# Fourier tables fetched during the fold, padded tails, softmax scaling on GpSimd, merge weights a tile ahead

## The chip, the cores and the metric

The kernel runs on one core of one Trainium2 chip. The metric is the device time of one execution in microseconds (us). A core has TensorE (PE, matrix products), VectorE (DVE), ScalarE (ACT), GpSimd (POOL) and SyncE (SP), which work side by side and wait for each other by semaphores. DMA transfers are issued from the queues of SP, ACT and POOL. Matrix products land in PSUM banks; GpSimd can't read these.

## What is computed

One layer of a transformer-like encoder over two sequences with shared weights: 1024 sample tokens and 256 prompt tokens, each with 16 learned meta tokens in front, width 1024.

```python
h = rms_norm(x, norm_mix_g)
q, k, v, f, g_attn, g_four = split(h @ w_in)       # 512, 128, 128, 512, 1024, 1024
q, k = axial_rope(head_rms_norm(q)), axial_rope(head_rms_norm(k))
a = softmax(q @ k.T * HEAD_DIM ** -0.5) @ v @ w_attn_o   # 8 query heads share 2 key heads
fo = real(fftn(f, axes=(positions, group channels), norm='ortho')) @ w_four_o
x = x + (sigmoid(g_attn) * a + sigmoid(g_four) * fo) @ w_out
x = x + (silu(gate) * up) @ w_ffn_out              # gate, up = rms_norm(x) @ w_ffn_in
return rms_norm(x, final_norm_g)                   # without the meta tokens
```

## The kernel before

Nearly every product of two matrices is done as three products of rounded parts: each operand is split into a high part (ScalarE copies it into a rounded format) and a low part (the difference, made by VectorE or GpSimd), and `three` (L224 to L231) adds high x high, high x low and low x high. So every fresh operand costs one copy and one subtraction before TensorE can use it, and these splits must stay ahead of TensorE.

On-chip memory is handed out by `Slots`: 27 single slots and 7 triples. A freed slot goes to the back of a line and the one freed longest ago is handed out first. A new holder's first writer waits for the old holder's last reader.

The order of the work. Up to the attention's start the framework orders the instructions of each engine itself, by the order in the program and its own estimate of the times. In attention, merge and the projection's start the order of TensorE, ScalarE and VectorE is the program's (`manual_schedule`), while that of GpSimd is still the framework's. Each engine runs its list strictly in order.

The stages that the change touches:

- **Fold.** The real Fourier transform uses the symmetry of cosine and sine: `folds` (L461) adds and subtracts mirrored positions of the normed input, for eight blocks k of 128 channels. GpSimd rebuilds the input from its parts (L488), VectorE makes sums and differences (L491, L492), and both are split (L494, L495) into the slots called eo.
- **Fourier input.** `fourier_in` (L500) multiplies the eight folded blocks with channel weights into six PSUM banks (L515 to L519): four banks of 128 positions, one of 41 and one of 128, the last and 9 rows of the fifth belonging to the prompt. Then ScalarE and VectorE split the banks into ue and uo (L539 to L545), bank after bank.
- **Position tables.** `fourier` (L611) multiplies ue and uo with tables of cosines and sines over positions: tabp for the prompt (fp, two tables of 128 and 41 rows, L649), then tabc and tabs for the sample (fs, five tables each, of 128, 128, 128, 128 and 9 rows, L666). There are five kinds of output (two blocks of cosines, a narrow one of four columns, two blocks of sines), with one half for fp and two halves for fs. The tables are fetched by DMAs on GpSimd's queue (L615, L672).
- **Gates as filler.** `gate_gen` (L553) computes the gate logits in groups: 12 weight units, and for each eight steps of three matmuls of 512 columns. `weave` (L146) mixes it with the main work: each `yield` of the main work names a cost in nominal ns, a share of it is added to a debt, and gate groups (a nominal 640 each for the first 512 positions) are emitted until it is paid. In `build` the shares are 0.6 in the Fourier stage, 0.35 in `q_pass` (queries) and 0.7 in `kv_pass` (keys and values). The gates of the other positions fill attention, with a cost per step in the table `FILL` (L551): "p" for the prompt's tiles, "s" for the sample's, "end" and "drain" for the last.
- **Attention.** Ten tiles of 128 queries in two groups of four heads; the two prompt tiles come first. For each head: scores into PSUM (L949), maximum on VectorE (L954), exponential on ScalarE with the row's sum (L961). One head later VectorE makes the reciprocal of the sum (L965) and scales the row (L966). From one head after the end of a group the rows are transposed on TensorE (L883), split (L885, L886) and multiplied with V (L903, L904).
- **Merge.** For each of eight tiles of 128 output channels: `need` (L1085) combines and splits the tile's weights, `fourier(i)` (L1106) makes the Fourier product one tile ahead of the attention product (loop from L1166), and both are joined with the sigmoid of the gates. The weights' DMAs are issued by `load` on SP.
- **Output projection.** `w_out` (L1218) is started by `next(then)` from inside the merge; its first weight unit is split at L1253, the low part by GpSimd.

After these come the second norm and the feed-forward network, which the change leaves as they are.

Of the kernel before, what the change touches and what calls it, by code (L numbers as in the profile page):

```python
# [10 lines left out]
F32R = mybir.dt.float32r  # L11
AF = mybir.ActivationFunctionType
ALU = mybir.AluOpType
# [4 lines left out]
P = 128  # L18
# [118 lines left out]
def f32(ap):  # L137
    return ap.bitcast(F32)
# [44 lines left out]
class Kernel:  # L183
# [313 lines left out]
            yield  # L497
        sl.put(*hs, ep, od)

    def fourier_in(self, ps):  # L500

        nc, sl = self.nc, self.sl
        cols = [(j * P, P) for j in range(4)] + [(512, 41), (553, P)]
        banks = [ps.tile([P, 512], F32, tag="mm" if j < 4 else "tr", name=f"u{j}") for j in range(6)]
        for k in range(KD):
            while k not in self.eo:
                next(self.fold)
            parts = self.eo.pop(k)
            w = [x[:, k % 2 * 512 : k % 2 * 512 + 512] for x in self.wc[k // 2]]
            for j, (b, m) in enumerate(cols):  # L510
                for odd, (h, l) in enumerate(parts):
                    s = slice(260, 512) if odd else slice(260)
                    out, hm, lm = banks[j][:m, s], h[:, b : b + m], l[:, b : b + m]
                    if k or odd:
                        nc.tensor.matmul(out, hm, w[0][:, s], start=False, stop=False)  # L515
                    else:
                        nc.tensor.matmul(banks[j][:m, :], hm, self.wz[:], start=True, stop=False)
                    nc.tensor.matmul(out, hm, w[1][:, s], start=False, stop=False)
                    nc.tensor.matmul(out, lm, w[0][:, s], start=False, stop=odd == 1 and k == KD - 1)  # L519
                yield 0  # L520
            for x in parts:
                sl.put(*x)
            if k + 2 < KD:
                next(self.fold)
            if k % 2:
                sl.put(*self.wc[k // 2])
        next(self.fold, None)
        ue = [sl.get("ue", F32R) for _ in range(3)]
        uo = [sl.get("uo", F32R) for _ in range(3)]
        for x in uo:  # L530
            nc.gpsimd.memset(f32(x.v(4, 256))[:, :, 252:256], 0.0)
        for j, (_, m) in enumerate(cols):
            ev = banks[j][:m, :260].rearrange("p (g c) -> p g c", g=4)
            b = j % 2 * 520
            u = ue[j // 2]
            for base, w, src in ((0, 64, ev[:, :, :64]), (256, 1, ev[:, :, 64:65])):
                hv = u.v(4, w, b + base)[:m]
                lv = u.v(4, w, b + 260 + base)[:m]
                nc.scalar.copy(hv, src)  # L539
                nc.vector.tensor_tensor(lv, src, f32(hv), op=ALU.subtract)  # L540
            b = j % 2 * 512
            u = uo[j // 2]
            src = banks[j][:m, 260:512]
            nc.scalar.copy(u[:m, b : b + 252], src)
            nc.vector.tensor_tensor(u[:m, b + 256 : b + 508], src, f32(u[:m, b : b + 252]), op=ALU.subtract)  # L545
        self.U = ue, uo
        yield 6000

    FILL = {"s": 455, "p": 350, "end": 480, "drain": 900}  # L551

    def gate_gen(self, chunks, lo_engine):  # L553

# [56 lines left out]
    def fourier(self, ps):  # L611
        nc, a, sl = self.nc, self.a, self.sl
        tp = [sl.get(f"tabp{j}", F32R) for j in range(2)]
        for j, m in enumerate((P, 41)):
            nc.gpsimd.dma_start(tp[j][:m, : 4 * NLP], a["pos_p"][j, :m])  # L615
        yield from self.fourier_in(ps)
        us = self.U

        def u_e(uu, j, m, p, part):
# [24 lines left out]
            nc.sync.dma_start(self.f_d[row : row + m, lo : lo + n], st[:m, :n])  # L644


        ms = [P, 41]
        for kind, p in kinds:
            rows = 4 if kind == "4" else P  # L649
            pf = ps.tile([P, 512], F32, tag="mm", name=f"fp{kind}{p}")  # L650
# [12 lines left out]
        sl.put(*tp)  # L663


        ms = [P, P, P, P, 9]  # L666
        tabs = {}

        def tab(name):
            tabs[name] = [sl.get("tab" + name, F32R) for _ in range(5)]  # L670
            for j, m in enumerate(ms):
                nc.gpsimd.dma_start(tabs[name][j][:m, :1040], a["pos_" + name][j, :m])  # L672

        tab("c")
        for i, (kind, p) in enumerate(kinds):
            if i == 1:
                tab("s")
            rows = 4 if kind == "4" else P
            tt = tabs["s" if kind == "o" else "c"]
            st = sl.get("fst")  # L680
# [170 lines left out]
    def attention(self, ps, tiles, tag_s, tag_v):  # L851
# [80 lines left out]
        for i, (t, g) in enumerate(units):  # L932
# [8 lines left out]
            for h in range(4):  # L941
# [21 lines left out]

                def scale(p=p, rc=rc, total=total):
                    nc.vector.reciprocal(rc, total)  # L965
                    nc.vector.tensor_scalar(p, p, rc, None, op0=ALU.mult)  # L966

                ps4.append(p)
                turns(1)
# [88 lines left out]
    def merge(self, then):  # L1058
# [105 lines left out]
        load(2)  # L1164
        load_gates(2)
        for i in range(8):  # L1166
            yield from fourier(i + 1)
            if i == 0:
                run_all(self.last_af)
# [7 lines left out]
            for c in (0, 2, 1):  # L1177
# [11 lines left out]
                    self.three(pm[:, :n], [(wk, mv)], k == 0, k == 3)  # L1189
                    yield 3 * n / 2.4  # L1190
                if c == 0:
                    need(i + 2)
                    load(i + 3)
                v = gt[:, n : 2 * n]
                nc.vector.tensor_tensor(v, pm[:, :n], v, op=ALU.mult)
# [8 lines left out]
                    sl.put(gt)  # L1204

                late.append(rows)
                if c == 2 and i == 7:
                    next(then)
            sl.put(w)
            if i < 4:  # L1210
# [7 lines left out]
    def w_out(self, tiles, ps, then=None, apart=False):  # L1218
# [31 lines left out]
        raw = sl.get("wo", F32, "s")  # L1250
        nc.sync.dma_start(raw[:, :1024], a["w_out"][0])
        yield 0
        units[0] = self.split(raw, 1024, "wo", nc.gpsimd, "s")  # L1253
        sl.put(raw)
        yield 0
        for half in range(2):
# [438 lines left out]
    def build(self):  # L1695
# [3 lines left out]
        with self.psum("pb", {"mm": 4, "tr": 2, "g": 2}) as ps:  # L1699
# [4 lines left out]
            def ahead(main, start, then):  # L1704
                for i, cost in enumerate(main):
                    if i == start:
                        next(then)
                    yield cost

            weave(ahead(self.fourier(ps), QSTART, q_pass), gates, 0.6)  # L1710
            weave(ahead(q_pass, KVSTART, kv_pass), gates, 0.35)
            weave(kv_pass, gates, 0.7)
            run_all(gates)
            self.free_hT(self.hT[0])
            gates = Filler(self.gate_gen([1, 2], self.nc.gpsimd))
# [193 lines left out]
```

## Time and profile before

| | |
|---|---|
| runs | 1735.22, 1735.85, 1737.88 us (median 1735.85) |
| the profiled execution | 1737.35 us, of which the span from first to last instruction is 1735.6 |
| mean granted TensorE clock | 0.988 of full speed |
| bytes moved | 195.77 MB, mean 113 GB/s |

How to read it: times count from the span's start. PE is TensorE's matmuls, PEld its weight loads, which overlap them; matmuls are pipelined, so starts, not lengths, tell the pace. A line's shape such as `9*128 9x260` is the stationary operand (9 rows, 128 columns) and the moving one (9 rows, 260 columns). A bracket in the order of time holds how long the engine stood before the instruction, and what ended that. In a row of waits stand the engine and line that waited, for whom, the us in total, the times and the longest. Tile names are those that the memory had first, so a table may be shown under the name of an earlier tile in the same triple. L numbers are lines of the kernel.

### The profile page before, as it was taken

The numbers are of one execution on the slowest core, as the hardware profiler recorded it, in microseconds if no ns is written. First come the engines' busy times: TensorE is split into PE (matmuls) and PEld (weight loads), VectorE is DVE, ScalarE is ACT, GpSimd is POOL, SyncE is SP. The second block draws the span as 40 slices with busy tenths as digits, with TensorE's granted clock in tenths as the row PEclk, the third lists the DMA queues.
The fourth block names the chain that finished last, engine by engine and source line by source line (L and its number), as shares of the span: only waits on it lengthen the run. The fifth ranks groups of instructions, "written<-read, shape, count | busy, mean of one in ns | idle before, by whom it ended". The sixth has DMA issues, their size and how long they took to land.

```text
span 1735.6 us, 25870 instructions
## 1 busy us (share of the span) xinstructions
PE 1672.8 (96%) x9789; PEld 1489.0 (86%) x9789; DVE 1137.2 (66%) x2086; ACT 723.0 (42%) x1462; POOL 299.7 (17%) x347
## 2 busy tenths in 40 slices
PE   7998999999999999989989999999999999999998
PEld 7897888877787878878879999999999998888886
DVE  5562454357888886652379766667666768665685
ACT  6432333355666666451355222222232224444444
POOL 3440233311002111663353000000000000000002
PEclk9997999999999999999999999999999999999999
DMA  6124232221111217534442222322232237553534
GB/s 245 39 106 134 100 122 91 80 79 57 44 59 45 67 56 231 169 108 143 150 166 77 86 69 95 102 90 83 94 102 90 70 119 256 196 182 101 159 98 152
DMA packets 90541, 195.77 MB, mean 113 GB/s; under 512 B 9773, under 2 KB 41161, under 8 KB 90416
## 3 DMA queue, kind: packets, MB, share of 16 engines
q1 hardware_dynamic: 80592, 176.88, 31.0%
q10 hardware_dynamic: 8400, 12.53, 2.0%
q0 software_dynamic: 1424, 4.70, 0.8%
q8 instruction: 77, 1.26, 0.3%
q14 instruction: 48, 0.39, 0.1%
HBM read 138.65 MB, written 55.42 MB: 112 GB/s over the span
## 4 chain that ended last, share of the span: by engine, by line
PE 60%; DVE 6%; issue 3%; ACT 3%; POOL 2%; DMA 1%; POOLq 0%; ACTq 0%; SPq 0%; DVEq 0%
PE i L231 10%; PE i L229 10%; PE i L230 10%; PE o L231 5%; PE o L230 5%; PE o L229 4%; PE S L949 3%; PE pt L883 2%; PE wo L230 1%; PE pv L903 1%; PE wo L231 1%; PE wo L229 1%; PE pv L904 1%; PE g L229 1%; POOL gt L1196 1%
## 5 line engine op out<-in xcount | busy, mean ns | idle before, releaser
L1402 ACT CAST w<-wi 128x512 fp32r<-128x512 f32 x168 | 104.0, 621 | 270.5 <-PE i L231 216.5
L229 PE MATMUL i<-A,w 128*128 128x384 f32 x616 | 208.6, 339 | 3.0 <-ACT w L1402 2.7
L231 PE MATMUL i<-A,w 128*128 128x384 f32 x616 | 208.4, 339 | 2.4 <-POOL w L1404 2.3
L230 PE MATMUL i<-A,w 128*128 128x384 f32 x616 | 208.2, 338 | 0.0
L229 PE MATMUL i<-Ah,w 128*128 128x256 f32 x616 | 173.6, 282 | 0.9 <-DVE sc L1458 0.7
L231 PE MATMUL i<-Ah,w 128*128 128x256 f32 x616 | 173.7, 282 | 0.0
L230 PE MATMUL i<-Al,w 128*128 128x256 f32 x616 | 173.3, 281 | 0.0
L238 POOL TENSOR_SCALAR fin0r<-fin0ss 128x1 f32<-128x1 f32 x1 | 0.8, 785 | 757.5 <-ACT X L246 757.5
L885 ACT CAST pT<-pt 128x512 fp32r<-128x512 f32 x156 | 90.5, 580 | 89.6 <-PE pt L883 87.6
L886 DVE TENSOR_TENSOR pT<-pt,pT 128x512 fp32r<-128x512 f32 x156 | 106.9, 686 | 26.9 <-ACT pT L885 25.1
L1404 DVE TENSOR_TENSOR w<-wi,w 128x512 fp32r<-128x512 f32 x154 | 105.3, 685 | 29.0 <-ACT w L1402 28.6
L229 PEld LDWEIGHTS i<-A,w 128*128 128x128 f32 x616 | 116.7, 190 | 3.6 <-ACT w L1402 2.9
L231 PEld LDWEIGHTS i<-A,w 128*128 128x128 f32 x616 | 116.5, 189 | 3.1 <-POOL w L1404 3.1
L229 PEld LDWEIGHTS i<-Ah,w 128*128 128x128 f32 x616 | 116.3, 189 | 1.6 <-DVE sc L1458 0.9
L230 PEld LDWEIGHTS i<-Al,w 128*128 128x128 f32 x616 | 116.5, 189 | 0.0
L230 PEld LDWEIGHTS i<-A,w 128*128 128x128 f32 x616 | 116.5, 189 | 0.0
L231 PEld LDWEIGHTS i<-Ah,w 128*128 128x128 f32 x616 | 116.4, 189 | 0.0
L954 DVE TENSOR_REDUCE sm<-S 128x1 f32<-128x1040 f32 (+1 forms) x80 | 86.4, 1080 | 41.0 <-PE S L949 35.1
L961 ACT ACTIVATE p<-S,sm 128x1040 f32<-128x1040 f32 (+1 forms) x80 | 80.1, 1001 | 35.3 <-DVE sm L954 30.9
L883 PE MATMUL pt<-ident,p 128*128 128x128 f32 (+1 forms) x624 | 93.7, 273 | 0.0
L231 PE MATMUL o<-wfo,act 128*128 128x512 f32 (+1 forms) x212 | 82.2, 388 | 1.6 <-DVE act L1536 1.6
L230 PE MATMUL o<-wfo,act 128*128 128x512 f32 (+1 forms) x212 | 82.1, 387 | 0.2 <-DVE wfo L1540 0.2
(734 smaller groups left out, 4470.5 us busy)
## 6 DMA issues: line engine op xcount, KB each, us to landing
wi<-w_fi SPq DMA_DIRECT2D x48, 512.0 KB
act_d<-sc SPq DMA_DIRECT2D x77, 192.0 KB
wg<-w_g SPq DMA_DIRECT2D x24, 512.0 KB
act<-act_d SPq DMA_DIRECT2D x37, 320.0 KB
wfo<-w_fo SPq DMA_DIRECT2D x21, 512.0 KB
X<-act_d SPq DMA_DIRECT2D x31, 320.0 KB
act_d<-sc SPq DMA_DIRECT2D x77, 128.0 KB
gt<-gate SPq DMA_DIRECT2D x32, 256.0 KB
```

Of the source, the lines that this page charges most:

```text
L229: mm(out, sh, mh, start=first and i == 0, stop=False)
L230: mm(out, sh, ml, start=False, stop=False)
L231: mm(out, slo, mh, start=False, stop=last and i == n - 1)
L883: nc.tensor.transpose(pt[:rows, h * P : (h + 1) * P], me.ps4[h][:, col : col + rows], self.ident[:])
L885: nc.scalar.copy(pT[:rows, :512], pt[:rows, :])
L886: nc.vector.tensor_tensor(pT[:rows, 512:1024], pt[:rows, :], f32(pT[:rows, :512]), op=ALU.subtract)
L903: nc.tensor.matmul(me.pv[:], vst, pT[:rows, :512], start=j == 0, stop=False)
L949: nc.tensor.matmul(S[:, base + lo : base + hi], hq, self.kT[seq][g][v][:, lo:hi], start=v == 0, stop=v == 1)
L954: nc.vector.tensor_reduce(nb, S[:, base : base + L], axis=AX.X, op=ALU.max, negate=True)
L961: self.last_exp = nc.scalar.activation(p, S[:, base : base + L], AF.Exp, bias=nb, accum_out=total)
L1402: nc.scalar.copy(w[:, :512], src)
L1404: eng.tensor_tensor(w[:, 512:1024], src, f32(w[:, :512]), op=ALU.subtract)
```

## The change

- The gates' first unit is loaded and split before the fold begins (`next(gates)`); the shares become 0.6, 0.28 and 0.62, and the last yield of `fourier_in` grows from 6000 to 8000.
- The ten sample tables are fetched from within the fold loop, as slots come free, instead of after `fourier_in`.
- The two short tables and the short bank are filled with zeros up to 128 rows, and their matmuls use all 128.
- `FILL`: "s" from 455 to 420, "p" from 350 to 500.
- The scaling of the exponentials moves from VectorE to GpSimd; the reciprocal stays.
- In the merge `need(i + 2)` is called before `fourier(i + 1)` instead of after the first product of tile i; in the last tile the first projection unit is split after the first product instead of the second, with its low part on VectorE.

```diff
@@ fourier_in
-    def fourier_in(self, ps):
+    def fourier_in(self, ps, tab):
...
             if k + 2 < KD:
                 next(self.fold)
+            elif k + 2 == KD:
+                next(self.fold, None)
+            for _ in range((0, 0, 2, 0, 2, 0, 4, 2)[k]):
+                tab()
             if k % 2:
                 sl.put(*self.wc[k // 2])
-        next(self.fold, None)
         ue = [sl.get("ue", F32R) for _ in range(3)]
         uo = [sl.get("uo", F32R) for _ in range(3)]
-        for x in uo:
+        for x in uo[:2]:
             nc.gpsimd.memset(f32(x.v(4, 256))[:, :, 252:256], 0.0)
+        nc.gpsimd.memset(f32(ue[2][:, :520]), 0.0)
+        nc.gpsimd.memset(f32(uo[2][:, :1024]), 0.0)
...
-        yield 6000
+        yield 8000
-    FILL = {"s": 455, "p": 350, "end": 480, "drain": 900}
+    FILL = {"s": 420, "p": 500, "end": 480, "drain": 900}
@@ fourier
-        for j, m in enumerate((P, 41)):
-            nc.gpsimd.dma_start(tp[j][:m, : 4 * NLP], a["pos_p"][j, :m])
-        yield from self.fourier_in(ps)
+        for j in range(2):
+            nc.gpsimd.dma_start(tp[j][:, : 4 * NLP], a["pos_p"][j])
+        tabs = {"c": [], "s": []}
+        def tab():
+            name = "c" if len(tabs["c"]) < 5 else "s"
+            j = len(tabs[name])
+            t = sl.get("tab" + name, F32R, "s")
+            tabs[name].append(t)
+            if j == 4:
+                nc.gpsimd.memset(f32(t[:, :1040]), 0.0)
+            m = P if j < 4 else 9
+            nc.gpsimd.dma_start(t[:m, :1040], a["pos_" + name][j, :m])
+        yield from self.fourier_in(ps, tab)
...
-        ms = [P, 41]
+        ms = [P, P]
...
-        ms = [P, P, P, P, 9]
-        tabs = {}
-        def tab(name):
-            tabs[name] = [sl.get("tab" + name, F32R) for _ in range(5)]
-            for j, m in enumerate(ms):
-                nc.gpsimd.dma_start(tabs[name][j][:m, :1040], a["pos_" + name][j, :m])
-        tab("c")
+        ms = [P] * 5
         for i, (kind, p) in enumerate(kinds):
-            if i == 1:
-                tab("s")
@@ attention
-                    nc.vector.tensor_scalar(p, p, rc, None, op0=ALU.mult)
+                    nc.gpsimd.tensor_scalar(p, p, rc, None, op0=ALU.mult)
@@ merge
         for i in range(8):
+            if i:
+                need(i + 2)
             yield from fourier(i + 1)
...
                 if c == 0:
-                    need(i + 2)
+                    if i == 0:
+                        need(2)
                     load(i + 3)
...
-                if c == 2 and i == 7:
+                if c == 0 and i == 7:
                     next(then)
@@ w_out
-        units[0] = self.split(raw, 1024, "wo", nc.gpsimd, "s")
+        units[0] = self.split(raw, 1024, "wo", nc.vector, "s")
@@ build
+            next(gates)
             weave(ahead(self.fourier(ps), QSTART, q_pass), gates, 0.6)
-            weave(ahead(q_pass, KVSTART, kv_pass), gates, 0.35)
-            weave(kv_pass, gates, 0.7)
+            weave(ahead(q_pass, KVSTART, kv_pass), gates, 0.28)
+            weave(kv_pass, gates, 0.62)
```

## The prediction

> **What bounds the kernel now.** I read the page first, then a table of stages, then TensorE's own waits, then the order of time around each hole.
>
> ```profile
> span 1735.6 us, 25870 instructions
> PE 1672.8 (96%) x9789; PEld 1489.0 (86%) x9789; DVE 1137.2 (66%) x2086; ACT 723.0 (42%) x1462; POOL 299.7 (17%) x347
> PEclk9997999999999999999999999999999999999999
> ```
>
> TensorE is busy 96% of the span, and the clock row dips in one slice. An edit can only fill TensorE's idle 63 us, win back halved clock, or shorten TensorE's own work. The table of stages (columns: length, then busy time of PE, PEld, DVE, ACT, POOL, then clock, DMA share, GB/s) shows where these lie.
>
> ```profile
> 127.50:136.30 8.80, 4.34 (x21) 3.24 (x19) 5.55 (x17) 4.80 (x19) 2.64 (x5) 0.95 0.98 336
> 136.30:155.66 19.36, 19.21 (x65) 15.67 (x66) 3.70 (x12) 2.71 (x6) 0.00 (x0) 0.50 0.19 56
> 155.66:336.00 180.34, 178.16 (x1008) 150.63 (x1007) 81.00 (x198) 55.00 (x130) 57.12 (x83) 1.00 0.29 100
> 336.00:343.55 7.55, 4.85 (x18) 3.69 (x19) 3.09 (x14) 2.82 (x11) 1.33 (x3) 0.77 0.68 244
> 400.00:680.00 280.00, 271.64 (x1624) 224.17 (x1625) 231.05 (x345) 180.85 (x327) 37.85 (x33) 1.00 0.23 71
> 777.00:787.30 10.30, 6.34 (x16) 4.75 (x16) 5.50 (x6) 5.11 (x6) 6.79 (x5) 0.67 0.75 257
> 787.30:1735.60 948.30, 931.86 (x5431) 859.23 (x5429) 638.04 (x1167) 331.48 (x640) 75.72 (x67) 0.99 0.37 121
> ```
>
> The diff touches nothing that runs after 787, so the last row stays and every microsecond won earlier arrives at the end. The holes are: before the table matmuls, with 19.36 us at half clock behind it; at the end of the K/V pass (336 to 343.55); thin ones in attention; and the start of the output projection (777 to 787.3). Between 155.66 and 336 TensorE waits for almost nothing, so what is won before it is carried through.
>
> **The hole before the table matmuls.** In order of time (start, length, engine, line, operation, in brackets the wait before it and what ended it):
>
> ```profile
> 126.41 1.14 ACT L571 CAST wgh<-wg 128x512 fp32r<-128x512 f32 x2 [1.65 <-DMA wg<-w_g]
> 126.81 0.29 PE L515 MATMUL u<-wch,eo 128*128 128x260 f32 x1
> 127.46 0.36 ACT L539 CAST ue<-u 128x256 fp32r<-128x256 f32 x1
> 131.44 0.40 PE L231 MATMUL g<-hT0h,wgl 128*128 128x512 f32 x1
> 135.88 0.36 ACT L539 CAST ue<-u 128x256 fp32r<-128x256 f32 x1
> 136.29 0.48 PE L229 MATMUL fpe<-hT0l,ue 128*128 128x136 f32 x1 [4.46 <-ACT ue L539]
> ```
>
> ScalarE copies six banks out from 127.46; the sixth, which the first table matmul needs, starts at 135.88: 8.4 us for five banks, 1.7 each. It starts late because ScalarE stood behind the gate weights' DMA (126.41). The sixth bank's own matmuls begin at 126.81 and end just before 127.7, so a bank takes about 0.7 us on TensorE and the first was complete near 126.81 - 4 x 0.7 = 124.0. With next(gates) the first gate unit is loaded and split before the folds; ScalarE can start near 124.1 and reach the sixth bank near 132.5. TensorE covers the time with gate groups: six ran in about 4.3 us (the busy 4.34 of the first row), 0.7 each. The yield of 8000 x 0.6 = 4800 buys eight of nominal 640, so cover lasts to 127.5 + 5.6 = 133.1. The idle 4.46 us falls to about 0.3: gain 4.2. So short a pause should not halve the clock (400 to 680 has 8.4 us of idle in pieces at clock 1.00), and the 19.36 us at 0.50 shrink by half less what was waiting in them: 9.5.
>
> The price is in the folds: the gates now hold three slots during them, and ten tables take slots as they come free, with their DMA issues and one or two memsets on POOL between its fold additions. More fold splits must then wait for TensorE to release the fold before last. It happens already:
>
> ```profile
> 97.43 0.77 ACT L494 CAST eo<-ep 128x681 fp32r<-128x681 f32 x1 [3.19 <-PE u L518]
> ```
>
> ScalarE waited 3.19 us there and TensorE did not, for it had a whole fold (six banks of 0.7, 4.2 us) in hand. For six folds I bound the cost by 0 and 0.7 each, 0 to 4, and take 0.5. The memsets of the padded ue and uo precede banks five and six only and have over 4 us: nothing. The tables already arrived before they were needed (the 136.29 row waits for ScalarE, not a DMA), so fetching them early gains nothing itself.
>
> **The tails.** The padded operand replaces a 9-row (or 41-row) matmul with one of 128 rows:
>
> ```profile
> 156.16 0.28 PE L231 MATMUL fse<-tabc,ue 128*128 128x260 f32 x1
> 156.28 0.28 PE L229 MATMUL fse<-tabc,ue 128*128 128x260 f32 x1
> ...
> 156.52 0.28 PE L231 MATMUL fse<-tabc,ue 128*128 128x260 f32 x1
> 156.73 0.38 PE L229 MATMUL fse<-tabc,ue 9*128 9x260 f32 x1
> 156.95 0.28 PE L230 MATMUL fse<-tabc,ue 9*128 9x260 f32 x1
> 157.07 0.28 PE L231 MATMUL fse<-tabc,ue 9*128 9x260 f32 x1
> 157.28 0.50 PE L229 MATMUL g<-hT0h,wgh 128*128 128x512 f32 x1
> 157.61 0.40 PE L230 MATMUL g<-hT0h,wgh 128*128 128x512 f32 x1
> ```
>
> Inside the tail the starts are 0.12 apart (156.95 to 157.07), as in full-height runs, so the rows cost nothing; but the step into it is 0.21 and the next 0.22, out of it 0.21 and 0.33 where a 512-column matmul takes 0.23 (0.69 for three). That is 0.09 + 0.10 + 0.09 + 0.10 = 0.38 us per tail. Twelve of the fifteen tails have 128 output columns: 12 x 0.38 = 4.6; I leave the three narrow ones out.
>
> **The end of the K/V pass.**
>
> ```profile
> 339.43 0.33 PE L790 MATMUL ktr<-ident,ks 128*128 128x128 f32 x1 [2.70 <-DVE ks L779]
> ```
>
> Gate work runs out here. There are 96 groups of 640, or 61440. Before, the three shares spend 26000 x 0.6 + 61000 x 0.35 + 34040 x 0.7 = 60778 ahead of the last yield, one group left. After: 28000 x 0.6 + 61000 x 0.28 + 34040 x 0.62 = 54985, ten left, and the last yield of 8000 x 0.62 places seven or eight, 5 us, over the 2.70 us wait. With it goes the half clock (0.77 over 7.55 us is 1.7 us lost). Gain 4.4. In the Q pass each tile gets one fifth less gate work, with no wait next in line.
>
> **Attention.** Four edits meet: scaling moves from VectorE to GpSimd, the filler rate for the short tiles rises 350 to 500, and for the long ones falls 455 to 420 (about 32 x 150 = 4800 against 120 x 35 = 4200 nominal, so the same work earlier).
>
> ```profile
> PE S L949 <- ACT p L961: 6.2, 10, 1.5
> PE pv L903 <- DVE ao L911: 5.2, 9, 0.9
> 482.48 0.15 DVE L965 RECIPROCAL sm<-sm 128x1 f32<-128x1 f32 x1
> 482.73 0.77 DVE L966 TENSOR_SCALAR p<-p,sm 128x1040 f32<-128x1040 f32 x1
> 484.36 0.60 PE L883 MATMUL pt<-ident,p 128*128 128x128 f32 x4
> L1016 POOL CAST pT<-x64r 4x1024 fp32r<-4x1024 f32 x3 | 3.1, 1034 | 15.2 <-DMA x64r<-w 15.1
> L214 POOL TENSOR_TENSOR wol<-wo,woh 128x1024 fp32r<-128x1024 f32 x14 | 34.5, 2472 | 47.0 <-ACT woh L213 46.3 <-issue 0.7
> ```
>
> TensorE is busy 271.64 of 280 us there, so VectorE's 0.77 us less per head can return at most a part of the waits of 6.2 and 5.2 us; both also hang on ScalarE. I take 1 us for these and 0.5 for the fill. The new cost is delay: the reciprocal ends at 482.63, and at a change of unit TensorE wants the scaled row at the transposes of the next head, 484.36: 1.73 us. GpSimd's price for the multiply isn't in the trace; the nearest rows are its one-input cast over 1024 columns, 1.03 us, and its two-input subtraction over 1024, 2.47 us. The multiply has one tensor input, so I take 1.1 to 1.3, inside the 1.73. Behind it on POOL stand the gate weights' low halves, wanted a unit later. Sum for attention 1.5, from +6 down to -12 (next part).
>
> **Merge and output projection.**
>
> ```profile
> PE fo L229 <- ACT wm L1095: 2.5, 4, 0.8
> PE fo L229 <- ACT pT L1095: 0.7, 1, 0.7
> PE fo L231 <- DVE wm L1096: 0.6, 4, 0.2
> PE wo L230 <- POOL wol L214: 2.3, 1, 2.3
> PE wo L229 <- ACT woh L213: 1.7, 1, 1.7
> ```
>
> Between 690 and 777 TensorE waits 3.8 us for split merge weights that are made in the tile before their use. A tile earlier they have a tile's length more (eight tiles in about 90 us): gain 3.5. VectorE and ScalarE may then stand at need() for the weights' DMA, with the sums of the first Fourier half queued behind; four PSUM banks cover that. The first projection unit, split after the first of tile 7's three products and on VectorE, is ready before TensorE ends the merge: 2.3 + 1.7 = 4.0 us go, and the half clock behind: (1 - 0.67) / 0.5 x 10.3 = 6.8 us at half speed, of which TensorE worked about 5.8, 2.9 lost. I keep 6.4 of the 6.9.
>
> **Sum.** 4.2 + 9.5 - 0.5 + 4.6 + 4.4 + 1.5 + 3.5 + 6.4 = 33.6 us. The profiled execution took 1737.35 for a span of 1735.6; the sum gives 1703.8 there. It stands 1.5 above the median of the runs, 1735.85, so the forecast is 1702.
>
> **Rivals.**
> *The first hole only narrows.* If the copies still start near 127.5 (a split of the second gate unit in front, or late slots), cover to 133.1 leaves 3.1 us idle before 136.29, and the clock falls again: 2.8 + up to 9.5 come back, 1712 to 1714. For it: ScalarE did take the second unit's split at 126.41. Against: that load is also issued earlier now. The clock in these rows fell after an idle 2.70 us too. The Trainium skill (TensorE: Matmul & The Clock Gate, Why this matters for your kernels) says that one idle window, gaps over about 3 us, halves the clock; by it 3.1 us would be on the edge and 2.70 safe, and the trace has 0.77 around the 2.70.
> *Scaling is late.* At the two-input 2.47 us it misses the 1.73 by 0.74 in each of 16 long units, 12 us: 1714. The Trainium skill (GPSIMD Engine Reference, Engine selection) says not to do elementwise work there, two-input operations being about half as fast as on VectorE but one-input ones near line rate; by it the multiply would be near the cast's price and the sum would stand, though no row here shows a one-input operation on all 128 rows.
> *The tails gain nothing* if the steps belong to the change of table rather than of height: 1707. Against: the table changes between 156.16 and 156.28 too, at 0.12.
> *POOL's queue turns against it, slower than before.*
>
> ```profile
> POOL wgl L572 <- ACT wgh L571: 207.0, 21, 29.4
> ```
>
> GpSimd stands 207.0 us, 10 at a time, at ScalarE's gate copies. It does so with nothing else to do; but if its fixed order puts such a wait ahead of a unit's last scaling, TensorE stands for most of it. It outweighs the 33.6 from four such waits in twenty units: 1742 with four, 10 us each. Against: the copy is issued within a step of its subtraction.
>
> **Numbers.** Forecast 0.62, narrowed hole 0.15, late scaling 0.11, tails 0.06, queue 0.04, the rest small gains lost together 0.02. Predicted 1702; low end 1692 (waits of attention recovered whole, no cost in the folds, more filler effect), high end 1716 (either of the two large rivals with its price). Faster by over 0.2%, about what measurement can tell: 0.94; slower 0.04; within 0.02.
>
> **What would show it.** Right: no idle over 1 us before the first table matmul and clock 1.00 from 127 to 345; 0.12 steps through the fifth table; no wait at the last K transposes; no wait of fo for wm; the projection's first matmul straight behind the merge. Wrong: a half-clock stretch near 140; transposes waiting for POOL; holes between 100 and 127 in the folds; a GpSimd multiply of 2 us or more.

## The result and the profile after

The changed kernel takes 1760.88 us (median of four runs, 1759.32 to 1762.57), the kernel before 1735.53 beside it: ratio 1.0144, 95% interval 1.0127 to 1.0162. It is 25 us slower; 34 us faster were forecast.

The page of the changed kernel, its span, its busy times and its clock row:

```profile
span 1760.8 us, 26129 instructions
PE 1673.6 (95%) x9789; PEld 1488.5 (85%) x9789; DVE 1090.9 (62%) x2008; ACT 722.3 (41%) x1462; POOL 498.2 (28%) x428
PEclk9999999999999899999999999999999999999999
```

TensorE is busy as long as before (1672.8), so nearly all of the loss is idle time. POOL has gone from 299.7 to 498.2 us, more than four times what VectorE gave up (1137.2 to 1090.9). The table of stages (columns as before):

```profile
130.00:137.00 7.00, 7.00 (x37) 5.85 (x36) 4.92 (x15) 4.39 (x15) 0.52 (x1) 1.00 0.74 217
137.00:157.00 20.00, 19.31 (x137) 16.86 (x137) 4.98 (x12) 3.48 (x7) 0.00 (x0) 1.00 0.43 143
157.00:322.00 165.00, 162.53 (x927) 139.02 (x924) 82.76 (x206) 55.45 (x135) 59.97 (x86) 1.00 0.30 102
323.80:704.30 380.50, 341.32 (x1928) 275.73 (x1929) 209.67 (x340) 210.02 (x395) 247.55 (x120) 0.97 0.21 65
704.30:805.70 101.40, 90.56 (x499) 79.76 (x498) 66.89 (x125) 50.95 (x104) 55.91 (x78) 0.98 0.48 152
805.70:1760.70 955.00, 938.24 (x5444) 864.03 (x5444) 644.86 (x1175) 335.35 (x645) 78.03 (x68) 0.99 0.37 122
```

The front went as forecast: no hole near 130, clock 1.00. The fourth row, attention, has 39.2 us in which TensorE does nothing, and a clock of 0.97. Cut at the first scores, the first Fourier product of the merge and the first projection product, the two spans compare like this:

| stage | before | after | difference | forecast |
|---|---|---|---|---|
| up to the first scores | 340.0 | 323.8 | -16.2 | -22.2 |
| attention | 340.8 | 380.5 | +39.7 | -1.5 |
| merge | 97.9 | 101.4 | +3.5 | -9.9 |
| projection to end | 956.9 | 955.1 | -1.8 | 0 |

What attention waits for (us in total, times, longest), and the price of the multiplication in the groups of lines:

```profile
POOL p L974 <- DVE sm L973: 99.7, 44, 12.0
PE S L957 <- ACT p L969: 16.6, 21, 7.3
PE pt L891 <- POOL p L974: 14.1, 15, 1.2
ACT pT L893 <- POOL wgl L577: 11.1, 2, 8.3
```

```profile
L974 POOL TENSOR_SCALAR p<-p,sm 128x1040 f32<-128x1040 f32 x64 | 187.1, 2925 | 87.5 <-DVE sm L973 74.0 <-PE pt L891 8.4 <-issue 2.9
```

GpSimd takes 2.925 us for what VectorE did in 0.77. One change of unit in order of time:

```profile
483.63 0.15 DVE L973 RECIPROCAL sm<-sm 128x1 f32<-128x1 f32 x1
483.97 2.92 POOL L974 TENSOR_SCALAR p<-p,sm 128x1040 f32<-128x1040 f32 x1 [0.92 <-DVE sm L973]
486.95 0.33 PE L891 MATMUL pt<-ident,p 128*128 128x128 f32 x1 [0.92 <-POOL p L974]
```

The reciprocal ends at 483.78, the multiplication starts 0.19 later, and the transposes start the moment it ends, 0.92 us after they could have.

### The profile page after: what moved, and what is told of

It is laid out like the page before. It is cut to its first block, busy times and chain, and to the rows that moved or that the text cites. A ratio compares the mean times of both kernels' runs of the same rounds, so it can differ in the third digit from the quotient of the medians.

```text
span 1760.8 us, 26129 instructions
## 1 busy us (share of the span) xinstructions
PE 1673.6 (95%) x9789; PEld 1488.5 (85%) x9789; DVE 1090.9 (62%) x2008; ACT 722.3 (41%) x1462; POOL 498.2 (28%) x428
## 4 chain that ended last, share of the span: by engine, by line
PE 59%; DVE 7%; POOL 7%; ACT 4%; issue 4%; DMA 2%; POOLq 0%; DVEq 0%; ACTq 0%; SPq 0%
PE i L231 10%; PE i L229 10%; PE i L230 10%; PE o L231 4%; PE o L230 4%; PE o L229 4%; POOL p L974 4%; PE S L957 3%; PE pt L891 2%; PE wo L230 1%; PE wo L229 1%; PE wo L231 1%; PE pv L911 1%; DVE sm L962 1%; PE g L229 1%
## 5 line engine op out<-in xcount | busy, mean ns | idle before, releaser
L974 POOL TENSOR_SCALAR p<-p,sm 128x1040 f32<-128x1040 f32 (+1 forms) x80 | 202.5, 2532 | 116.5 <-DVE sm L973 99.7
L894 DVE TENSOR_TENSOR pT<-pt,pT 128x512 fp32r<-128x512 f32 (+1 forms) x138 | 94.7, 687 | 90.0 <-ACT pT L893 89.7
L893 ACT CAST pT<-pt 128x512 fp32r<-128x512 f32 (+1 forms) x138 | 80.1, 581 | 109.5 <-PE pt L891 96.0
L891 PE MATMUL pt<-ident,p 128*128 128x128 f32 (+1 forms) x624 | 99.2, 278 | 14.4 <-POOL p L974 14.1
L891 PEld LDWEIGHTS pt<-ident,p 128*128 128x128 f32 (+1 forms) x624 | 74.1, 136 | 29.9 <-POOL p L974 18.0
```

Of the source, the lines that this page charges most:

```text
L891: nc.tensor.transpose(pt[:rows, h * P : (h + 1) * P], me.ps4[h][:, col : col + rows], self.ident[:])
L893: nc.scalar.copy(pT[:rows, :512], pt[:rows, :])
L894: nc.vector.tensor_tensor(pT[:rows, 512:1024], pt[:rows, :], f32(pT[:rows, :512]), op=ALU.subtract)
L974: nc.gpsimd.tensor_scalar(p, p, rc, None, op0=ALU.mult)
```

## The experiments

Differences below are between medians; the median of before moved by 1.2 us from one set of runs to another. The theory was that the price of the multiplication on GpSimd makes the loss in attention; its rivals were the filler rates, and a loss only through lateness at the changes of unit.

**One part back, one part alone.** In the changed kernel the multiplication goes back to VectorE:

```diff
-                    nc.gpsimd.tensor_scalar(p, p, rc, None, op0=ALU.mult)
+                    nc.vector.tensor_scalar(p, p, rc, None, op0=ALU.mult)
```

> The changed kernel with one word put back: the multiplication runs on VectorE again. Theory (the price of the multiplication on GpSimd is what attention lost: 2.92 us against VectorE's 0.77): attention falls from 380.5 us back to the 341 it had before, and the time to 1721 (1760.9 - 39.7). Rival (the new filler rates 420 and 500 starve the long tiles, the multiplication only shifts where it waits): 1750 to 1760, and TensorE goes on waiting in attention. Rival (the multiplication costs only its lateness at the sixteen unit changes, 14 us of waits of the transposes): 1745, and the waits of the scores for the exponentials stay.

Measured: 1726.51 us, 34.4 less than the changed kernel, attention 344.9. The reverse line in the kernel before:

> The kernel before with this one word changed: the multiplication on GpSimd. Theory (price): 1775 (1735.5 + 39.7), attention about 380 us. Rival (filler rates): 1736 to 1745, since the rates are the old ones. Rival (lateness at unit changes only): 1750.

Measured: 1766.04, ratio 1.0177 (1.0162 to 1.0192), attention 371.0. This one line makes the kernel slower by about 30 us by itself, with the old rates; the theory holds, at 30 to 34 us and not 39.7. Two more runs take the rest of the change apart. The merge as before:

```diff
-            if i:
-                need(i + 2)
             yield from fourier(i + 1)
...
-                    if i == 0:
-                        need(2)
+                    need(i + 2)
...
-                if c == 0 and i == 7:
+                if c == 2 and i == 7:
...
-        units[0] = self.split(raw, 1024, "wo", nc.vector, "s")
+        units[0] = self.split(raw, 1024, "wo", nc.gpsimd, "s")
```

> The multiplication on VectorE and the merge as before (weights folded in the tile before, projection unit split on GpSimd after the last product); front stages and filler rates as changed. Theory (the earlier fold of merge weights itself lengthened the merge by the 3.5 us that the trace shows): 3 to 4 us faster than the run with the multiplication on VectorE alone, 1717. Rival (my sum: the fold a tile ahead saves 9.9 us, and only GpSimd's backlog from attention hid it): 10 us slower than that run, 1731.

Measured: 1726.62, the same as with the merge edits (1726.51). Both expectations missed: in the whole the edits neither cost 3.5 nor save 9.9. The stages show why: the merge is longer with them, 102.3 us for 99.1, and what follows it shorter, 954.1 for 956.1. Then the filler rates as before too:

```diff
-    FILL = {"s": 420, "p": 500, "end": 480, "drain": 900}
+    FILL = {"s": 455, "p": 350, "end": 480, "drain": 900}
```

> As the run before it, and the filler rates are the old ones too: what is left of the change is the front (tables during the fold, gates first, shares, padded tails). Theory: the front brings the 16.2 us that the trace shows up to the first scores: 1719. My sum had 22.2 there: 1713. The difference to the run before it is the rates alone: theory nothing (within 2 us); my sum half a microsecond.

Measured: 1720.97 (one of its six runs took 1730.75, the others 1719.28 to 1723.90). The front alone is worth 15.8 us; the rates, which I took for nothing, cost 5.7 (attention 339.8 to 346.5 us). Front -15.8, rates +5.7, merge -0.1, multiplication +34.4 make +24.2, against 25.3 measured. As each part was taken off the run before it, they add up by construction; what is left over is the movement of the median of before. In the kernel before, with nothing else changed, the multiplication cost less, 29.3.

**Late, or too busy?** Only the fourth head of each unit, the last before the transposes, is scaled on VectorE:

```diff
-                def scale(p=p, rc=rc, total=total):
+                def scale(p=p, rc=rc, total=total, e=nc.vector if h == 3 else nc.gpsimd):
                     nc.vector.reciprocal(rc, total)
-                    nc.gpsimd.tensor_scalar(p, p, rc, None, op0=ALU.mult)
+                    e.tensor_scalar(p, p, rc, None, op0=ALU.mult)
```

> The changed kernel with the multiplication of every unit's fourth head on VectorE, the other three heads on GpSimd. Theory (lateness: what costs is that the last row of a unit is scaled too late for the transposes): the waits of the transposes for GpSimd go and nearly all of the 34.4 us between the changed kernel and the one with VectorE come back, 1727 to 1733. Rival (occupancy: GpSimd's queue delays the gate halves and the slots, by as much as it is busy): a quarter of the multiplications goes and so does a quarter of the 34.4, 1752.

Measured: 1737.48. A quarter of the multiplications taken away brought back 23.4 of the 34.4 us, and the transposes no longer wait for GpSimd at all. So two thirds of the loss is lateness of one multiplication in four. Left are 11 us, which neither expectation gave. The stage of attention, with VectorE alone and in this run (columns as before):

```profile
322.90:667.80 344.90, 328.99 (x1928) 268.57 (x1929) 264.67 (x420) 210.55 (x395) 47.03 (x40) 1.00 0.23 72
323.00:676.20 353.20, 330.03 (x1929) 269.42 (x1929) 222.62 (x360) 209.95 (x395) 198.10 (x100) 0.99 0.23 70
```

TensorE is idle for 15.9 us in the first row and 23.2 in the second; in the changed kernel it was 39.2. So the late multiplications made 16.0 us of idle time, 14.1 of them the direct waits, and 11.3 us of busy time (341.3 for 330.0), at a clock of 0.97 for 0.99. The scores wait for the exponentials nearly as long without them, 14.7 us for 16.6 (6.9 with VectorE alone), most of the difference to VectorE in one hole (GpSimd and ScalarE in order of time):

```profile
519.67 2.38 POOL L1027 TENSOR_TENSOR hT0l<-x64r,hT0l 4x1024 fp32r<-4x1024 f32 x1
522.15 2.92 POOL L974 TENSOR_SCALAR p<-p,sm 128x1040 f32<-128x1040 f32 x1
525.04 1.26 POOL L577 TENSOR_TENSOR wgl<-wg,wgh 128x512 fp32r<-128x512 f32 x1
526.33 0.58 ACT L893 CAST pT<-pt 128x512 fp32r<-128x512 f32 x1 [7.21 <-POOL wgl L577]
```

The low half of a gate unit stands behind a multiplication and the Fourier tails (the rows of four that `fourier` leaves over); ScalarE waits 7.21 us for the slot that it frees, and the scores behind it 6.2. The changed kernel has the same hole, 8.3 and 7.3 us. So the tails went to VectorE:

```diff
-                nc.gpsimd.tensor_copy(t[b : b + 4, :], r[b : b + 4, :n])
+                nc.vector.tensor_copy(t[b : b + 4, :], r[b : b + 4, :n])
...
-            nc.gpsimd.tensor_tensor(t[x, :], r[x, :n], f32(t[x, :]), op=ALU.subtract)
+            nc.vector.tensor_tensor(t[x, :], r[x, :n], f32(t[x, :]), op=ALU.subtract)
```

> The kernel with the fourth head's multiplication on VectorE (1737.5), and the eight operations on the 4-row Fourier tails (six casts and two subtractions of 0.75 to 2.4 us, which GpSimd took between 509 and 522 us) on VectorE too. Theory (the 11 us that this kernel still loses to VectorE alone are mostly one hole: the tails push a multiplication and a gate half back, and ScalarE waits 7.2 us for the slot of that half): the hole of 520 to 530 us goes, 6.2 us of wait and about 3 of half clock, 1728. Rival (the loss is spread over all units, with the waits of the scores for the exponentials): 1735 to 1738.

Measured: 1735.12, 2.4 less. The hole at 520 is gone (TensorE busy 17.38 of 520 to 540, where it was 13.41), but attention is 352.6 us long and was 353.2: the time was lost again elsewhere. Of the remaining 8.6 us, 5.3 stand in the trace as waits of the scores for the exponentials, spread out now (12.2 us in 20 waits, none over 2.0; 6.9 in 11 with VectorE alone). Why the exponentials come later stays open.

**What the price is.** The changed kernel with a constant as the factor:

```diff
-                    nc.gpsimd.tensor_scalar(p, p, rc, None, op0=ALU.mult)
+                    nc.gpsimd.tensor_scalar(p, p, 0.5, None, op0=ALU.mult)
```

> The changed kernel, the multiplication on GpSimd by a constant 0.5 and not by the column of reciprocals: the softmax's denominators are left out. Theory (a column read for each partition makes the multiplication cost like a two-input operation, and with a constant it goes at the rate of the one-input cast): the multiplication takes 1.0 to 1.4 us and the time is near that of VectorE, 1727. Rival (any 128-row operation on 1040 columns has this price on GpSimd): 2.9 us and 1761.

Measured: 1737.12, the multiplication 2.850 us in the median. It isn't the column. The time falls all the same, for a multiplication that needs no reciprocal starts behind the exponentials and ends earlier: the transposes don't wait for GpSimd here either, and 23.8 us come back, as with the fourth head on VectorE. GpSimd is nearly as busy in attention as in the changed kernel (241.4 us for 247.6), so it was not its work as such that cost them. Then a price list, eleven operations behind the last product of the best kernel so far:

> The best kernel so far (1713.5) with eleven operations of GpSimd added behind its last product, on 1040 columns, most on 128 rows: two memsets, casts, multiplications by a constant and by a column, two-input multiplications. Only their durations count. Theory (the forecast took the price of one-input work from a row on 4 rows, and that row was no measure for 128): the cast on 128 rows takes 2.0 us or more, the one on 4 rows 1.0. Rival (the cast is 1.0 on 128 rows too, and the multiplication alone is slow): 1.0 against 2.9. Rival (what is slow is the rounding to the matmul's format): the operations into plain 32-bit take half of those into that format.

```profile
L1793 POOL TENSOR_SCALAR wfo<-bx 128x1040 fp32r<-128x1040 f32 x1 | 3.0, 3049 | 0.1
L1795 POOL TENSOR_SCALAR by<-bx 128x1040 f32<-128x1040 f32 x1 | 2.9, 2922 | 0.1
L1792 POOL TENSOR_SCALAR by<-bx 128x1040 f32<-128x1040 f32 x1 | 2.9, 2855 | 0.0
L1794 POOL TENSOR_SCALAR by<-bx 4x1040 f32<-4x1040 f32 x1 | 2.8, 2837 | 0.1
L1796 POOL TENSOR_TENSOR by<-by,bx 128x1040 f32<-128x1040 f32 x1 | 2.4, 2372 | 0.1
L1791 POOL CAST wfo<-bx 4x1040 fp32r<-4x1040 f32 x1 | 1.9, 1921 | 0.1
L1790 POOL CAST wfo<-bx 128x1040 fp32r<-128x1040 f32 x1 | 1.1, 1057 | 0.0
L1789 POOL COPY by<-bx 128x1040 f32<-128x1040 f32 x1 | 1.1, 1050 | 0.1
```

Rows 1 and 3 are by a constant (row 1 rounded to the matmul's format), row 2 by a column, row 4 on 4 rows. Copy and cast on 128 rows take 1.05, so the 1.03 of the cast on 4 rows in the kernel before had been a good measure for them; the cast on 4 rows here took 1.92, a single instruction, and why is open. Neither the rows, nor the rounding (0.2), nor the column (0.07) is the cause of the multiplication's price: a multiplication by a scalar is 2.7 times a copy and dearer than the two-input one, 2.37. The first rival of this expectation was right. The Trainium skill (GPSIMD Engine Reference, Engine selection) puts two-input elementwise work there at about half of VectorE's speed and one-input work near line rate; the copy, 1.05 where VectorE's multiplication of the same size takes 0.77, comes near that, the multiplication by a scalar, 2.92, does not.

**The front.** Short tails again, in the front-only kernel:

```diff
-        ms = [P] * 5
+        ms = [P, P, P, P, 9]
...
-            if j == 4:
-                nc.gpsimd.memset(f32(t[:, :1040]), 0.0)
```

(and the same for the two tables of 41 rows and for the folded operands)

> The front-only kernel (1721.0) with the tables' tails at 9 and 41 rows again, everything else kept. My sum: twelve tails at 0.38 us come back, 4.6 us slower, 1725.6. Rival (the tails gain nothing, the steps of the starts are taken up by other work): 1721. Rival (the memsets that pad stand in GpSimd's way during the folds): 1 to 2 us faster, 1719.

Measured: 1726.09, 5.1 slower; the sum said 4.6. The starts show the steps that the sum went by; the short tail in this run:

```profile
142.24 0.28 PE L231 MATMUL fse<-tabc,ue 128*128 128x260 f32 x1
142.45 0.38 PE L229 MATMUL fse<-tabc,ue 9*128 9x260 f32 x1
142.67 0.28 PE L230 MATMUL fse<-tabc,ue 9*128 9x260 f32 x1
```

With the padded tail the starts stay 0.12 apart to the end of the fifth table. The end of the K/V pass, in the front-only kernel:

```profile
314.24 4.29 SPq L869 DMA_DIRECT2D qT<-q_d  x2
318.58 0.42 SPq L869 DMA_DIRECT2D hT0l<-q_d  x1
322.84 0.79 PE L957 MATMUL S<-kTp,qT 128*128 128x272 f32 x2 [2.44 <-DMA qT<-q_d]
```

The last K transposes no longer wait, but the first scores wait 2.44 us for the queries, whose load begins at 314.24, when a slot of the K/V pass comes free. More gate work for the end:

```diff
-            weave(kv_pass, gates, 0.62)
+            weave(kv_pass, gates, 0.55)
```

> The front-only kernel (1721.0) with the gate share of the K/V pass 0.55 for 0.62: 34040 x 0.07 = 2383 nominal, 3.7 groups of 0.69 us, are left for the end of the pass, in front of the first scores. Theory (the first scores waited 2.44 us for their queries' load, whose slot frees only at the end of the K/V pass, and the half clock of 1.7 us followed): the wait is covered, 1717. Rival (work moved from one place to another gives nothing, the load lands later by as much): 1721.

Measured: 1717.30, 3.7 faster, and no wait for that load is left.

The best kernel so far (the front, this share, and the projection unit of the next part; VectorE scales, old rates) is 1713.52. In it the tables are loaded after the folds:

```diff
-            for _ in range((0, 0, 2, 0, 2, 0, 4, 2)[k]):
-                tab()
...
+        for _ in range(10):
+            tab()
         us = self.U
```

> The best kernel so far (1713.5) with the ten table loads after the last fold and not during the folds. Theory (the tables' slots, loads and memset held up the fold splits by the 2.1 us by which the fold products end later): those products end 2 us earlier, and if the tables come in time 1711.5. Rival (the two gate units in front of the folds hold them up, the tables cost nothing): the products end as late, and 1713.5, or more if the table products then wait for their tables.

Measured: 1713.42, no difference, and the fold products end as late. So the tables aren't what holds up the folds, nor do they gain. What holds them up is the gates in front, taken away here in the fastest kernel (1705.60, from the part on the merge below):

```diff
-            next(gates)
             weave(ahead(self.fourier(ps), QSTART, q_pass), gates, 0.6)
```

> The fastest kernel so far (1705.6) without the step that loads and splits the first gate units ahead of the folds; shares, yield, tables and tails as in it. My sum: the folds end 2 us earlier, the hole of 4.5 us in front of the first table product and half clock behind it come back: 9.5 + 4.2 less 2.1, 11.6 us slower, 1717. Rival (the longer cover behind the folds, 8000 for 6000, did it, and the early gate units only cost the 2.1 us): 1703.5.

Measured: 1710.92, 5.3 slower. The folds end 2.4 us earlier (126.8 for 129.2), and a hole is back in the same place. It has another wait than in the kernel before: the filler itself waits for the low half of its first gate unit.

```profile
131.06 0.80 PE L231 MATMUL g<-hT0h,wgl 128*128 128x512 f32 x1 [3.55 <-DVE wgl L577]
```

From 131.06 to 137 us the clock is 0.51, and 1.00 right behind, where the kernel before stayed at 0.50 for 19.36. So the step counts for about half of the 11.6 that I expected from it, since the half clock behind this hole lasts 6 us and not 19; why it lasted longer in the kernel before stays open.

**The merge.** Why did the edits give nothing? TensorE's waits there with them (multiplication on VectorE):

```profile
PE fo L1126 <- ACT fst L1139: 5.9, 4, 2.1
PE wo L229 <- ACT woh L213: 1.3, 1, 1.3
```

The waits for the weights are gone but for 1.9 us in front of the first tile, as forecast; in their place TensorE waits for ScalarE to empty the Fourier banks. In order of time:

```profile
717.33 1.41 POOL L1207 TENSOR_TENSOR gt<-gt 128x512 f32<-128x512 f32 x1 [1.36 <-DVE gt L1206]
717.50 1.52 DVE L1099 TENSOR_TENSOR wmf<-wmf 128x256 f32<-128x256 f32 x1
718.94 0.41 DVE L1100 TENSOR_TENSOR wmf<-wmf 128x256 f32<-128x256 f32 x1
719.39 0.62 ACT L1103 CAST ml<-wmf 128x512 fp32r<-128x512 f32 x1 [2.98 <-DVE wmf L1100]
722.31 0.75 ACT L1139 COPY fst<-fo 128x328 f32<-128x328 f32 x2
722.78 0.60 PE L1126 MATMUL fo<-hT0l 68*128 68x328 f32 x1 [2.00 <-ACT fst L1139]
```

VectorE's sum of 0.41 us takes 1.52, as long as GpSimd's addition runs; ScalarE stands 2.98 us at it, with the bank copies behind in its order. First try: the weights behind the Fourier products (and no longer behind the tile's first product, but for tile 0), in the front-only kernel, with the edits of the projection unit:

```diff
             yield from fourier(i + 1)
+            if i:
+                need(i + 2)
```

> The front-only kernel (1721.0) with the merge edits, but the weights of two tiles ahead are folded behind the Fourier products of the next tile and not in front of them; the first projection unit as in the change. Theory (in the change the weights' sums on VectorE stood in front of the copies that free the Fourier banks, 5.9 us of waits and two windows of half clock, which ate the gain): with the copies in front the waits for the weights (3.3) and for the projection unit (4.0, less 1.3 that stayed) and the half clock behind it (about 3) are all won: 1712. Rival (VectorE is the bound of the merge, whatever the order): 1721.

Measured: 1715.57, 5.4 faster, which is the projection unit: its wait falls from 5.4 to 1.3 us and the clock there, 0.66 over 10 us in the front-only kernel, stays at 1.00. The waits for the weights stay (2.7 us at the cast), now that the weights stand behind the copies. This and the K/V share together:

> What paid, together: the front of the change, the first projection unit early and on VectorE, the gate share of the K/V pass 0.55; the multiplication on VectorE, the old filler rates. Theory (the parts lie in different stages and add): 1721.0 - 5.4 - 3.7 = 1711.9. Rival (what the K/V pass won is given back in attention, which then has fewer gate groups): 1715.6.

Measured: 1713.52; of the 3.7 the share brings 2.1 here. Second try, in that kernel: casts in front as in the change, the two sums one product earlier, clear of GpSimd's addition:

```diff
+            if i:
+                need(i + 2)
             yield from fourier(i + 1)
-            if i:
-                need(i + 2)
...
+                if c == 1:
+                    sums(i + 3)
                 nc.vector.tensor_tensor(v, pm[:, :n], v, op=ALU.mult)
```

(`sums` holds the two VectorE sums that `need` began with; for tiles 0 to 2 they stay there)

> The best kernel so far (1713.5) with the merge weights cast in front of the Fourier products as in the change, but their two sums on VectorE one product earlier, in front of the last merge product's multiplication and so clear of GpSimd's addition behind it. Theory (in the change the sum of 0.41 us took 1.52 while GpSimd's addition ran, ScalarE stood 3.0 us at it, and the copies that free the Fourier banks came late by that): the bank waits of 5.9 us do not come, the waits for the weights (3.3) go, 1710. Rival (the casts in front of the copies are late by themselves): bank waits of 3 us or more, 1714 to 1717.

Measured: 1705.60, 7.9 faster still. The sums' durations (min/median/max, ns) in the kernel with the change's order and in this one:

```profile
L1099 DVE TENSOR_TENSOR wmf<-wmf x8: 406/1516/1520, 655.1 to 743.8; 128x256 f32<-128x256 f32 x8
```

```profile
L1098 DVE TENSOR_TENSOR wmf<-wmf x8: 406/418/425, 648.8 to 726.6; 128x256 f32<-128x256 f32 x8
```

One bank wait of 1.1 us is left, and none for the weights of the tiles behind the first; the merge takes 92.4 us. This run moves the sums and the casts at once against the kernel it starts from. But against the change's own merge only the sums have moved: its edits brought 0.1 there, and bring 5.4 + 7.9 = 13.3 here, if the parts add up. This version beats both kernels: ratio to before 0.9822 (0.9805 to 0.9839).

**The filler rates.** Only the short tiles' rate raised, in the front-only kernel (`"p": 350` to 500):

> The front-only kernel (1721.0) with only the filler rate of the short tiles raised, 350 to 500; the long tiles keep 455. Theory (the 5.7 us that both new rates cost come from the short tiles, where gate work is spent that was needed to cover waits later): 1726 or a little more, for the gates then run out earlier too. Rival (the cost is the long tiles' lower rate, 420 not covering the exponentials): 1719 to 1721.

Measured: 1723.45, +2.5 of the 5.7; the other 3.2 fall to the long tiles' 420 by difference, if the two add up; it was not run alone. And the long tiles' rate raised in the best kernel so far (`"s": 455` to 490):

> The best kernel so far (1713.5) with the long tiles' filler rate raised from 455 to 490. Theory (the lower rate, 420, cost about 3 of the 5.7 us, since the scores then wait longer for the exponentials): the waits shrink and the time falls by 1 to 3 us, unless the gates run out before the end. Rival (455 lies at the optimum): 1713 to 1716.

Measured: 1720.27, 6.8 slower. The trace shows what the higher rate does: the gates run out before attention ends. Their last product, then the last transposes, and the stretch behind:

```profile
653.34 0.28 PE L231 MATMUL g<-hT2h,wgl 128*128 128x256 f32 x1
655.62 0.66 PE L891 MATMUL pt<-ident,p 128*128 128x128 f32 x4 [1.09 <-DVE pT L894]
659.33 1.02 PE L891 MATMUL pt<-ident,p 128*16 128x128 f32 x4 [2.59 <-DVE pT L894]
660.00:670.00 10.00, 7.87 (x23) 5.79 (x22) 6.52 (x10) 5.89 (x9) 0.00 (x0) 0.50 0.78 243
```

In the best kernel the last gate product starts at 659.49, with attention's end at 659.6, these transposes wait for nothing, and the clock stays at 1.00. The short tiles' rate does the same in small: its last gate product starts at 659.24, 8 us before attention's end, the last transposes wait 2.4 us, and the clock is 0.83 from 660 to 680. So neither direction pays, and gate work that is spent early is missing at attention's end. With both new rates of the change the gates last to the end; how the lower rate of the long tiles costs its 3.2 stays open.

## Why the prediction was wrong, point by point

- **Attention, the step that failed:** "The multiply has one tensor input, so I take 1.1 to 1.3, inside the 1.73." It took 2.92, above what I had set as its upper bound, the two-input 2.47. Counting inputs picked the wrong row: the price goes with the operation.
- **The rival "scaling is late"** had the place right, the sixteen changes of unit, and the direct wait nearly: 12 us forecast, 14.1 measured. That number is partly luck, for with the price that was measured its own working gives 16 x (2.92 - 1.73) = 19. And it let each late microsecond cost one: taking the late multiplications away brought back 23.4, for TensorE's busy time had grown by 11.3 beside the waits, at a clock of 0.97 for 0.99. So the range missed even with this rival in it: by the table attention makes 41 of the 59 us between forecast and result.
- **"POOL's queue turns against it"** was the slower rival, and a part of it came, by another wait than the one that it names. GpSimd hardly stood at ScalarE's gate copies any more (1.4 us in attention); it was ScalarE that waited 8.3 us for a gate half behind multiplications. Taking the tails out of that queue gave 2.4 us. What it can claim lies in the 11 us that the fourth head on VectorE left, and how much of them stays open.
- **The fill at +0.5** was wrong by 6: equal nominal work isn't equal cover. Only for the short tiles' part, 2.5, do the traces show a cause.
- **The first hole (4.2 + 9.5):** filled, clock 1.00, as forecast. By itself the gate step brings 5.3, where the sum gives 4.2 + 9.5 less what the folds lose; the rest of the front's gain can't be put down to it alone.
- **The folds at 0.5:** 2.3 us (129.7 for 127.4 at their last product), inside the bounds of 0 to 4. The cause named, too, was only half right: the gates, not the tables.
- **The tails at 4.6:** 5.1, right, and by the steps that were named.
- **The K/V end at 4.4:** the wait for the K rows went, but the step did not ask what is late next: the queries' load, 2.44 us, with a clock of 0.66 from 320 to 330 in the changed kernel. Four more groups bring 3.7.
- **The merge at 9.9:** 0.1. The clause "four PSUM banks cover that" failed: a wait of 2.98 us in front of ScalarE's bank copies reached TensorE as 2.00. 5.9 us of bank waits and two stretches of 10 us at clock 0.83 ate the gain. The projection unit by itself brings 5.4, near its 6.4; the weights bring 7.9, more than their 3.5, once the casts stand in front and the sums run clear of GpSimd.
- **Nothing after 787 changes:** right, 956.9 and 955.1.

## What to carry to other kernels

Price an operation that moves to another engine by the same operation on that engine, or leave the range open above: a row with as many inputs isn't enough. What stands last before TensorE's next step is priced with what hangs on it; here 14 us of direct waits cost 23. And before a load or sum is put ahead of something, read the order of its engine behind the new place: a bank copy that had been in time there ate all that the earlier weights saved.

## What was not expected of the hardware

- GpSimd on 128 x 1040: copy 1.05 us, two-input multiplication 2.37, multiplication by a constant 2.86, by a column 2.92; on 4 rows the multiplication takes no less, 2.84.
- A VectorE sum with both operands in SBUF takes 1.52 us for 0.41 when a GpSimd addition started 0.17 before it, and ends 0.28 us after that addition. The Trainium skill (SBUF — State Buffer, Who interferes with whom) says that a VectorE instruction with two SBUF inputs contends with a GpSimd instruction that reads SBUF and that the later one is blocked fully; the rows agree nearly, for blocked fully the sum would end 0.41 after the addition; the version whose sums run clear of it, its casts in front, was 7.9 us faster.
- How long TensorE stays slow after a pause differs: an idle 2.44 us (the queries' load in the front-only kernel) was followed by a clock of 0.50 over 2.76 us and then 1.00, an idle 3.55 by 0.51 over 5.94, an idle 4.46 by 0.50 over 19.36. What decides it no run here shows.
